# A two-layer diffusion trunk on one core: the context's out projection in one plain fp32 pass, and two modulation blocks moved to the end of the first MoE

## The chip, the cores and the metric

The kernel runs on one core of one Trainium2 chip. The metric is the device time of one execution in microseconds (us), the median over several executions. TensorE (PE), VectorE (DVE), ScalarE (ACT), GpSimd (POOL) and SyncE (SP) each work through a queue of their own in order; SP here only issues transfers (DMAs), and POOL nearly only that.

## The reference

Two layers; each has a mixer (attention, retention and a gated recurrence side by side, then one out projection) and a mixture of 16 experts. 512 latent tokens pass through both layers; 256 context tokens need the full way only in layer 0. What the change touches, cut down:

```python
# modulation, per layer: six vectors of 1024 for the latents and six for the context
sh1, sc1, g1, sh2, sc2, g2 = split(silu(c) @ mod_w[i] + mod_b[i], 6)
h = rms(x, norm1_g[i]) * (1 + sc1) + sh1
mix = concat([att, ret, lru]) @ w_out[i]          # 1024 x 1024, latents and (layer 0) context
x = x + g1 * mix                                  # all of it in float32
x = x + g2 * experts(rms(x, norm2_g[i]) * (1 + sc2) + sh2)
```

## The kernel before, in words

**Split products.** Large projections are computed in `fp32r`, a cheaper matmul format: each operand is split into a rounded high part (ACT copy) and the remainder (DVE subtract), and `mm3` (L414) adds three products, high by high, high by low and low by high. Weights are split by `split` (L406, lines L410 and L411 of the trace, tile `ws`); mixer outputs by `mix_split` (L905). Other matmuls take plain fp32 operands, without a split: the experts, the router, the gates of the recurrence (L554, L555).

**Out projection.** The mixer leaves its result transposed: `mx_l` (8 feature blocks of 128 by 512 latents) and `mx_c` (8 by 256 context tokens). Output columns go in four groups of 256. Because feature blocks 4 and 5 come last, the projection is in two runs: `out1` (L985) over blocks 6, 7, 0, 1, 2, 3 for all four groups, and `out2` (L1003) over blocks 4, 5, which also transposes the finished tokens (L1022), forms the router's logits (L1031) and sums squares (L1001). Each run adds its product, times the gate, onto the tokens (`out_unit`, L901 and L903). The latents go first; the context then goes through both runs again with weights loaded and split anew.

**Order around it.** `outer` (L1123) does the latents' `out2`, then their `route` (softmax, top-k in rounds of MAX8, FIND_INDEX8 and MATCH_REPLACE8 on DVE, L1090 to L1093, then small PE transposes L1100 and L1101 and the index list `gl`), then the context's projection, then the first experts. The scaled tokens `xo` (L1075) are written to DRAM (`xh_l`) and gathered back by index (`gath`, L1189), transposed (`gT`, L1198), and feed gate and up matmuls of expert 0 (`gu`, L1236). The frame the kernel is built in has a scheduler: it orders every engine's queue itself by priority and data, so the context's projection and the latents' routing interleave.

**Modulation.** `mod_block` (L265) makes one of the six vectors: eight loads of 512 KB on SP, four pairs of them multiplied (macc, L276) with a DVE add after each pair (L279). It is cut into steps, and `hook` (L425) puts one step into each projection unit of a mixer, as long as steps are left. Layer 0's mixer does its own blocks 2 to 5 and layer 1's 0 and 1; layer 1's mixer does its own 2 to 5, that is 16 steps.

**Weights of the experts.** `load_experts` (L1208) asks for 2 MB pieces on SP as the nine buffers of a ring come free. After the first MoE, layer 1 reads its tokens back (`load_x`, L342), norms them (L357, L363, L365), transposes (L374) and starts its first projection (`pf`).

Of the kernel before, what the change touches and what calls it, by code (L numbers as in the profile page):

```python
# [12 lines left out]
F32 = mybir.dt.float32  # L13
# [7 lines left out]
P = 128  # L21
L = 512
# [32 lines left out]
RP_QG, RP_QP, RP_KG, RP_KP, RP_LAM, RP_DEC, RP_N = 0, 64, 128, 192, 256, 512, 520  # L55
PR = {"ev": 0, "macc": 0, "tmp": 0, "aT": -60, "rw": 20, "rs": 20}
XW = 776
SW = 771
# [7 lines left out]
class Trunk:  # L66
# [198 lines left out]
    def mod_block(self, m, c):  # L265
# [3 lines left out]
        for k0 in range(0, KD, 2):  # L269
            acc = self.pj("macc")  # L270
            for k in range(k0, k0 + 2):
                wt = self.t(("mw", "mw", "k4")[self.mj % 3], [1024], "mw")
                self.mj += 1
                nc.sync.dma_start(wt, a["mod_w"][i, c, k])
                for q in range(4):
                    nc.tensor.matmul(acc[32 * q:32 * q + 32, :256], self.scT[:, k, :], wt[:, q * 256:(q + 1) * 256],  # L276
                                     start=k == k0, stop=k == k0 + 1)
            with self.pr("macc"):
                nc.vector.tensor_tensor(rs, rs, acc[:, :256], op=ALU.add)  # L279
            if k0 < KD - 2:  # L280
                yield
        n, v = divmod(c, 3)
        if v == 2:
            nc.sync.dma_start(m["gr"][n], rs)
        else:
            pt = self.pj("mT")
            for bb in range(2):
# [4 lines left out]
            for s in range(2):  # L292
# [3 lines left out]
                else:  # L296
                    nc.vector.tensor_copy(o, pv[:, :, :, s])
        yield
# [588 lines left out]

    def out_unit(self, g, tp, ks, w, g1, xs):
        nc = self.nc
        p = self.pj("op")  # L890
        hi, lo = self.ms[tp // 2]
        for n, k in enumerate(ks):
            for t in range(2):
                o = (tp % 2) * 256 + t * P
                self.mm3(p[:, t * 256:(t + 1) * 256], hi[:, k, o:o + P], lo[:, k, o:o + P],
                         w[n][:, 0], w[n][:, 1], n == 0 and t == 0, n == len(ks) - 1 and t == 1)
        o = g * 256
        tmp = self.t("q2", [2, 256], "tmp")
# [5 lines left out]

    def mix_split(self, s, a, b):  # L905
        src = (self.mx_l, self.mx_c)[s][:, a:b]
        hi, lo = (x[:, a:b] for x in self.ms[s])
        self.nc.scalar.activation(flat(hi), flat(src), AF.Copy)  # L908
        self.nc.vector.tensor_tensor(flat(lo), flat(src), flat(hi).bitcast(F32), op=ALU.subtract)  # L909

    def mixer(self, i, m, mn, xsrc, xres):
# [60 lines left out]
        g1 = self.gate1(m, ctx)  # L972
        self.ms = [[self.t("big", [KD, L], "m" + w, F32R) for w in "hl"]]
        xs = self.load_x(*xres, nc.gpsimd, ctx=False)
        tabs = self.ret_tables((2, 3), [self.t("w6", [1536], "tab") for _ in range(2)])
        self.ret_core(1, kq1, tabs, ctx)
        for k in (6, 0, 2):
            self.mix_split(0, k, k + 2)
        for n, _ in enumerate(self.out1(i, 0, xs[:4], g1)):
            if n == 3:  # L980
                self.flush()
                self.mix_split(0, 4, 6)
        return xs, g1

    def out1(self, i, s, xs, g1):  # L985
        nc, a = self.nc, self.a
        K1 = [6, 7, 0, 1, 2, 3]
        for g in range(4):
            w = []
            for h in range(2):  # L990
                raw = self.t("mw" if h else "w4", [3, 256], "wo")
                nc.sync.dma_start(raw, a["wo1"][i, g, h])
                w += [self.split(raw[:, k], k, "ws") for k in range(3)]
            for tp in range(2 * s, 2 * s + len(xs) // 2):
                self.out_unit(g, tp, K1, w, g1, xs)
                yield
# [6 lines left out]
    def out2(self, i, s, xs, g1):  # L1003
        nc, a = self.nc, self.a
        tps = range(2) if s == 0 else range(2, 3)
        nt = len(xs)
# [3 lines left out]
        for g in range(4):  # L1010
            if g % 2 == 0:
                raw = self.t("xsl" if i == DEPTH - 1 else "w4", [2, 2, 256], "wo")
                nc.sync.dma_start(raw, a["wo2"][i, g // 2])
            w = [self.split(raw[:, g % 2, k], k, "ws") for k in range(2)]
            for tp in tps:
                self.out_unit(g, tp, (4, 5), w, g1, xs)
            if g == 3:
# [105 lines left out]
    def outer(self, i, m, xs, xsrc, g1, free, base_l, base_c):  # L1123
# [118 lines left out]

    def experts(self, i, m, st, first, base_l, base_c):
        nc = self.nc
# [33 lines left out]
        if late is not None:  # L1278
            late()
        self.fixed = False  # L1280

    def pe(self, ins):
# [61 lines left out]
def emit(ctx, tc, a, out):  # L1344
# [4 lines left out]
    for i in range(DEPTH):  # L1349
        last = i == DEPTH - 1  # L1350
        base = (out, None) if last else (k.xr_l, k.xr_c)
        with ExitStack() as cw:
# [22 lines left out]
            k.open(cw, b=(4, 1), d=(2, 1))  # L1375
            k.experts(i, ms[i], st, xl, *base)
        src = base
# [90 lines left out]
```

## Time and profile before

| what | us |
|---|---|
| median of 3 executions | 2016.27 (2015.25 to 2017.24) |
| profiled execution, its time | 2015.42 |
| its span, first to last instruction | 2013.7 |
| PE busy | 1824.0 |
| DVE busy | 823.0 |
| ACT busy | 586.4 |

Layer 0's mixer fills the span to about 480 us, the context's projection and routing lie at 480 to 560, the first MoE at 560 to 1076, layer 1's mixer up to about 1530, and the second MoE after it. In the trace a plain fp32 matmul appears as two records (the experts' 32 gate and up matmuls as x64), an fp32r matmul as one. A bracket behind a row gives the idle time of its engine just before it and what ended that.

### The profile page before, as it was taken

To read this page: it belongs to the slowest core of one execution; us is meant where nothing else is said; L and a number is where in the kernel's file an instruction comes from. 1 tells how busy PE (TensorE), PEld (TensorE's weight loads), DVE (VectorE), ACT (ScalarE), POOL (GpSimd) and SP (SyncE) were. 2 spreads that over 40 slices of the span, in tenths; PEclk is the share of its full clock that TensorE was granted. 3 is DMA by queue.
4 is the path that set the end of the run, shared out by engine and by line. 5 is a ranking of instruction groups with operands and counts; after the bars stand their busy time and mean duration, and the time that the engine had idled before them with its cause. 6 is when DMAs were issued, how large, how long until landed. Compare 5 with 4: busy or idle time off the path is not lost.

```text
span 2013.7 us, 28802 instructions
## 1 busy us (share of the span) xinstructions
PE 1824.0 (91%) x11900; PEld 1058.1 (53%) x11900; DVE 823.0 (41%) x2016; ACT 586.4 (29%) x1240; POOL 119.2 (6%) x118
## 2 busy tenths in 40 slices
PE   6999999999799999999996989999985997878776
PEld 5788888677433333333333778986762422222222
DVE  5797876676610101011104597976752100000000
ACT  5656465424210101011103565554330000000000
POOL 0000000000010111011000000000000000000000
PEclk9999999999699999999997989999987999999999
DMA  8352433246499999999985543211448999999997
GB/s 311 131 188 83 160 113 112 83 161 254 165 373 403 404 402 404 411 403 402 397 348 191 176 149 104 73 33 58 177 192 355 417 417 417 423 417 416 424 418 275
DMA packets 76403, 545.62 MB, mean 271 GB/s; under 512 B 8720, under 2 KB 15008, under 8 KB 51952
## 3 DMA queue, kind: packets, MB, share of 16 engines
q1 hardware_dynamic: 61312, 501.26, 62.6%
q0 software_dynamic: 14960, 42.53, 7.1%
q8 instruction: 93, 1.52, 0.3%
q14 instruction: 38, 0.31, 0.0%
HBM read 522.25 MB, written 21.50 MB: 270 GB/s over the span
## 4 chain that ended last, share of the span: by engine, by line
PE 36%; issue 29%; DMA 21%; DVE 7%; ACT 3%; POOL 3%; POOLq 0%; SPq 0%; ACTq 0%; DVEq 0%
DMA w<-wu 6%; DMA w<-wg 6%; DMA w<-wd 4%; PE gu L1236 4%; PE pt L416 3%; PE pt L418 2%; PE pt L417 2%; PE ao L839 2%; PE pf L416 2%; PE pf L417 2%; PE pf L418 2%; DMA xh_l<-xo 2%; PE ro L727 2%; PE macc L276 2%; PE oe L1321 1%
## 5 line engine op out<-in xcount | busy, mean ns | idle before, releaser
L1236 PE MATMUL gu<-w,xsT 128*64 128x512 f32 x2048 | 476.4, 617 | 50.6 <-DMA w<-wu 32.8
L1236 PEld LDWEIGHTS gu<-w,xsT 128*64 128x64 f32 x2048 | 153.4, 142 | 350.9 <-issue 271.0
L1321 PE MATMUL oe<-w,hid 128*64 128x512 f32 x1024 | 234.6, 610 | 9.7 <-ACT hid L1306 9.6
L1240 DVE TENSOR_TENSOR hid<-hid,gu 128x512 f32<-128x512 f32 x32 | 22.0, 687 | 462.9 <-ACT hid L1239 462.9
L1239 ACT ACTIVATE hid<-gu 128x512 f32<-128x512 f32 x32 | 19.1, 597 | 526.0 <-PE gu L1236 526.0
L1321 PEld LDWEIGHTS oe<-w,hid 128*64 128x64 f32 x1024 | 74.3, 140 | 157.1 <-issue 138.6
L417 PE MATMUL pt<-ws,hh 128*128 128x256 f32 x448 | 127.9, 285 | 5.0 <-DVE ws L411 5.0
L416 PE MATMUL pt<-ws,hh 128*128 128x256 f32 x448 | 130.8, 292 | 0.0
L418 PE MATMUL pt<-ws,hl 128*128 128x256 f32 x448 | 128.1, 286 | 0.0
L1324 DVE SCALAR_TENSOR_TENSOR ob<-oe,afl,g 128x512 f32<-128x512 f32 x32 | 24.0, 751 | 221.4 <-PE oe L1321 221.4
L1293 PE MATMUL guc<-w,xsT 128*32 128x512 f32 x1024 | 113.2, 594 | 0.0
L410 ACT ACTIVATE ws<-wraw 128x256 fp32r<-128x256 f32 x192 | 72.8, 411 | 83.6 <-PE pt L418 31.9
L416 PEld LDWEIGHTS pt<-ws,hh 128*128 128x128 f32 x448 | 85.8, 191 | 9.1 <-issue 8.6
L411 DVE TENSOR_TENSOR ws<-wraw,ws 128x256 fp32r<-128x256 f32 x192 | 76.7, 419 | 33.6 <-ACT ws L410 33.2
L417 PEld LDWEIGHTS pt<-ws,hh 128*128 128x128 f32 x448 | 85.7, 191 | 5.7 <-DVE ws L411 5.5
L418 PEld LDWEIGHTS pt<-ws,hl 128*128 128x128 f32 x448 | 85.8, 191 | 0.1
L1205 ACT ACTIVATE xsT<-gT,ab 128x128 f32<-128x128 f32 x80 | 36.6, 458 | 144.2 <-PE gT L1198 116.8
L416 PE MATMUL op<-ws,mh 128*128 128x256 f32 x256 | 74.9, 293 | 3.1 <-ACT mh L908 3.1
L817 ACT ACTIVATE p<-sc,mx 128x768 f32<-128x768 f32 (+1 forms) x80 | 65.2, 816 | 33.9 <-DVE mx L815 30.5
L417 PE MATMUL op<-ws,mh 128*128 128x256 f32 x256 | 74.0, 290 | 0.0
L418 PE MATMUL op<-ws,ml 128*128 128x256 f32 x256 | 73.5, 289 | 0.3 <-DVE ml L909 0.3
L815 DVE TENSOR_REDUCE mx<-sc 128x1 f32<-128x768 f32 (+1 forms) x80 | 66.4, 847 | 10.8 <-PE sc L811 10.2
(385 smaller groups left out, 3187.1 us busy)
## 6 DMA issues: line engine op xcount, KB each, us to landing
w<-wg SPq DMA_DIRECT2D x63, 2048.0 KB, 26.4
w<-wd SPq DMA_DIRECT2D x63, 2048.0 KB, 22.9
w<-wu SPq DMA_DIRECT2D x62, 2048.0 KB, 16.1
mw<-mod_w SPq DMA_DIRECT2D x80, 512.0 KB, 4.3
wraw<-w_in SPq DMA_DIRECT2D x48, 512.0 KB, 3.6
wo<-wo SPq DMA_DIRECT2D x24, 384.0 KB, 3.5
mw<-mod_a SPq DMA_DIRECT2D x16, 512.0 KB, 10.7
xh_l<-xo POOLq DMA_DIRECT2D x8, 512.0 KB, 12.4
```

What stands on the lines that cost most here:

```text
L276: nc.tensor.matmul(acc[32 * q:32 * q + 32, :256], self.scT[:, k, :], wt[:, q * 256:(q + 1) * 256], start=k == k0, stop=k == k0 + 1)
L410: nc.scalar.activation(t[:, 0], src, AF.Copy)
L411: nc.vector.tensor_tensor(t[:, 1], src, t[:, 0].bitcast(F32), op=ALU.subtract)
L416: nc.tensor.matmul(out, lh, rh, start=first, stop=False)
L417: nc.tensor.matmul(out, lh, rl, start=False, stop=False)
L418: nc.tensor.matmul(out, ll, rh, start=False, stop=last)
L727: nc.tensor.matmul(ol[64 * h:64 * h + 64, :], v, ws[h][:, :L], start=t == 0, stop=t == 5)
L815: nc.vector.tensor_reduce(mx, s[:, :n], axis=AX.X, op=ALU.max, negate=True)
L817: nc.scalar.activation(ptl[m][:, :n], s[:, :n], AF.Exp, bias=mx, accum_out=sm[:, m, t:t + 1])
L1236: self.pe(nc.tensor.matmul(d[64 * h:64 * h + 64, j, :], xl[:, k, x0:x0 + CAPL], W(j, k)[:, h * 512:(h + 1) * 512], start=k == 0, stop=k == ...
L1293: self.pe(nc.tensor.matmul(dc[32 * q:32 * q + 32, :], xc[:, k, c0:c0 + CAPC], W(q // 2, k)[:, (q % 2) * 512:(q % 2) * 512 + 512], start=k ...
L1321: self.pe(nc.tensor.matmul(o[64 * h:64 * h + 64, :], hid[:, 1, c * P + hh * 64:c * P + hh * 64 + 64], W(2, k)[:, h * 512:(h + 1) * 512], s ...
```

## The change

It has two parts, which share only the file.

1. The context's projection no longer splits anything. `out_unit_c` loads the weights of a group (three pieces: 384, 384 and 256 KB) and runs all eight feature blocks in one accumulation of plain fp32 matmuls, then one gated add. The context's `out1` run, its 16 half-tensor splits and its 32 weight splits are gone, and so is the buffer `mc`. 192 fp32r matmuls of 256 columns become 64 plain ones.
2. Blocks 2 and 3 of layer 1's modulation leave layer 1's mixer. `mod_bulk` computes them at the end of the first MoE: four loads of 2 MB into the experts' buffers, 32 matmuls each in one accumulation, one add each. Layer 1's mixer has 8 steps left.

```diff
+    def mod_bulk(self, m, cs):
+        for c in cs:
+            rs = self.t("ob", [512], "mrow")[:, :256]
+            nc.gpsimd.dma_start(rs, a["mod_b"][i, c])
+            acc = self.b("macc")
+            for h in range(2):
+                wt = self.t(WTAGS[i - 1][self.nw % len(WTAGS[i - 1])], [4, D], "mwt")
+                self.nw += 1
+                nc.sync.dma_start(wt, a["mod_w"][i, c, 4 * h:4 * h + 4].rearrange("k p e -> p k e"))
+                for k in range(4 * h, 4 * h + 4):
+                    for q in range(4):
+                        nc.tensor.matmul(acc[32 * q:32 * q + 32, :256], self.scT[:, k, :],
+                                         wt[:, k % 4, q * 256:(q + 1) * 256], start=k == 0, stop=k == KD - 1)
+            nc.vector.tensor_tensor(rs, rs, acc[:, :256], op=ALU.add)
+            self.mod_out(m, c, rs, self.b)
...
     def side_work(self, m, mn):
-        for c in range(2, 6):
+        for c in range(2 if mn is not None else 4, 6):
             yield from self.mod_block(m, c)
...
+    def out_unit_c(self, i, g, g1):
+        w = []
+        for h in range(2):
+            raw = self.t("mw" if h else "w4", [3, 256], "wo")
+            nc.sync.dma_start(raw, a["wo1"][i, g, h])
+            w += [raw[:, k] for k in range(3)]
+        raw = self.t("ring", [2, 256], "wo")
+        nc.sync.dma_start(raw, a["wo2"][i, g // 2][:, g % 2])
+        w += [raw[:, k] for k in range(2)]
+        p = self.pj("op")
+        for n, k in enumerate(K1 + K2):
+            for t in range(2):
+                nc.tensor.matmul(p[:, t * 256:(t + 1) * 256], self.mx_c[:, k, t * P:(t + 1) * P], w[n],
+                                 start=n == 0 and t == 0, stop=n == KD - 1 and t == 1)
+        self.residual(g, 2, p, g1)
...
         for g in range(4):
+            if s:
+                self.out_unit_c(i, g, g1)
+            else:
...
-            mc = self.t("big", [2, KD, C], "mc", F32R)
-            self.ms.append([mc[:, 0], mc[:, 1]])
...
-            if s:
-                for k in (6, 0, 2, 4):
-                    self.mix_split(1, k, k + 2)
-                for _ in self.out1(i, 1, x, g1):
-                    pass
...
         self.fixed = False
+        if mn is not None:
+            self.mod_bulk(mn, (2, 3))
```

`mod_out` is the tail of `mod_block` made a function: block 2 (a gate) is stored to DRAM (`gr`) by SP, block 3 is transposed and copied. `residual` is the tail of `out_unit`.

The queues of instructions, as the scheduler leaves them, at the three places that the prediction speaks of. **DVE, the start of the latents' top-k**, before (`ws` is a split weight, `tmp` and `xc` the context's gated add, `tk`, `iu` and `pw` belong to the top-k):

```order
L1090 MAX tk_5459<-pw_5451 48x8
L411 TENSOR_TENSOR ws_5724<-wo_5722,ws_5724 128x256
L1091 MAX_INDEX iu_5460<-tk_5459,pw_5451 48x8
L411 TENSOR_TENSOR ws_5727<-wo_5722,ws_5727 128x256
L1093 MATCH_REPLACE pw_5451<-tk_5459,pw_5451 48x256
L411 TENSOR_TENSOR ws_5730<-wo_5722,ws_5730 128x256
```

and now:

```order
L945 TENSOR_TENSOR xc_5145<-xc_5145,tmp_5541 128x2x256
L1133 MAX_INDEX iu_5459<-tk_5458,pw_5450 48x8
L1135 MATCH_REPLACE pw_5450<-tk_5458,pw_5450 48x256
L126 COPY xT_972_5547<-xT_971_5544 128x256
L1132 MAX tk_5458<-pw_5450 48x8
```

Between the first MAX and the last of the eight rounds there were 11 splits of weights; none is left, and of the gated adds two pairs are there instead of five.

**SP, the loads of the context's weights** (`wo`) among the experts' first weights (`w`) and the write of the latents (`xr_l`), before:

```order
L992 DMA wo_5711<-wo 128x768
L1223 DMA w_5949<-wu 128x4096
L1184 DMA xr_l<-xl_4488 128x1024 x4
L992 DMA wo_5722<-wo 128x768
L1013 DMA wo_5775<-wo 128x1024
L1013 DMA wo_5853<-wo 128x1024
L1223 DMA w_5951<-wd 128x4096
```

and now:

```order
L1258 DMA w_5704<-wu 128x4096
L1219 DMA xr_l<-xl_4488 128x1024 x4
L925 DMA wo_5602<-wo 128x768
L925 DMA wo_5604<-wo 128x768
L925 DMA wo_5642<-wo 128x768
L925 DMA wo_5644<-wo 128x768
L1258 DMA w_5706<-wd 128x4096
```

The loads of groups 0 and 1 now stand ahead of these rows; those of groups 2 (wo_5602, wo_5604) and 3 wait for PE to be done with groups 0 and 1, and the down weights `wd` stand behind them.

**SP, the end of the first MoE**, before (`xl` and `xc` are layer 1's tokens, `wraw` its first weights):

```order
L1223 DMA w_8564<-wd 128x4096
L403 DMA wraw_8973<-w_in 128x1024
L403 DMA wraw_8975<-w_in 128x1024
L171 DMA gw_9276<-gatew 128x1024
L268 DMA mrow_9017<-mod_b 128x256
L403 DMA wraw_9123<-w_in 128x1024
L403 DMA wraw_9125<-w_in 128x1024
L274 DMA mw_9060<-mod_w 128x1024
L274 DMA mw_9106<-mod_w 128x1024
L342 DMA xl_8788<-xr_l 128x1024 x4
```

and now:

```order
L1258 DMA w_8319<-wd 128x4096
L296 DMA mwt_8500<-mod_w 128x4x1024
L296 DMA mwt_8518<-mod_w 128x4x1024
L296 DMA mwt_8541<-mod_w 128x4x1024
L296 DMA mwt_8559<-mod_w 128x4x1024
L308 DMA gr_98<-mrow_8497 128x256
L365 DMA xl_8629<-xr_l 128x1024 x4
L365 DMA xc_8630<-xr_c 128x1024 x2
L426 DMA wraw_8814<-w_in 128x1024
L426 DMA wraw_8816<-w_in 128x1024
```

The reads of the tokens now stand behind the store of block 2's result, and layer 1's first weights behind the tokens. On POOL the row of `mod_b` for block 3 stands ahead of the last scatter into the context.

## Rows read from the trace of the kernel before

**Rows 1.** Windows by stage: context stage, first MoE. Columns as named in the answer's head.
```profile
480.00:560.00 80.00, 65.06 (x343) 41.71 (x343) 47.28 (x187) 22.53 (x57) 8.36 (x13) 0.79 0.64 236
560.00:1076.00 516.00, 515.13 (x3733) 186.91 (x3731) 63.22 (x118) 57.86 (x119) 57.10 (x40) 1.00 0.98 389
```

**Rows 2.** Timeline of PE in the context stage: start, duration, engine, line, operation, idle.
```profile
488.69 0.28 PE L416 MATMUL op<-ws,mc 128*128 128x256 f32 x1
...
495.10 0.28 PE L416 MATMUL op<-ws,mc 128*128 128x256 f32 x1
...
504.77 0.58 PE L416 MATMUL op<-ws,mc 128*128 128x256 f32 x1 [4.63 <-ACT ws L410]
```

**Rows 3.** Timeline of ACT in the context stage.
```profile
503.26 1.15 ACT L1075 ACTIVATE xo<-xl,n2r 128x1024 f32<-128x1024 f32 x1 [7.44 <-DMA xh_l<-xo]
```

**Rows 4.** DVE by line, 497 to 524 us: count, busy us, mean ns, idle before.
```profile
L411 DVE TENSOR_TENSOR ws<-wo,ws 128x256 fp32r<-128x256 f32 x11 | 4.4, 404 | 4.6 <-ACT ws L410 4.6
...
L1090 DVE MAX8 tk<-pw 48x8 f32<-48x256 f32 x8 | 3.3, 412 | 0.0
L1091 DVE FIND_INDEX8 iu<-tk,pw 48x8 uint32<-48x256 f32 x8 | 3.3, 410 | 0.0
L1093 DVE MATCH_REPLACE8 pw<-tk,pw 48x256 f32<-48x256 f32 x7 | 2.8, 401 | 0.0
```

**Rows 5.** Timeline of all engines, from the latents' index list to expert 0.
```profile
530.95 1.01 POOL L1189 DMA_INDIRECT gath<-xh_l,gl  x1 [25.71 <-DVE gl L1116]
...
537.99 1.94 PE L1198 MATMUL gT<-ident,gath 128*128 128x128 f32 x8 [3.48 <-DMA gath<-xh_l,gl]
...
541.46 7.11 PE L1236 MATMUL gu<-w,xsT 128*64 128x512 f32 x18 [0.98 <-ACT xo L1075]
...
549.78 9.66 PE L1236 MATMUL gu<-w,xsT 128*64 128x512 f32 x44
```

**Rows 6.** Timeline of PE in layer 1: plain fp32 matmuls with a full 128x128 operand.
```profile
1148.30 0.60 PE L555 MATMUL gate<-u,gw 128*128 128x259 f32 x2
1148.74 1.02 PE L554 MATMUL gate<-u,gw 128*128 128x512 f32 x2
```

**Rows 7.** Windows in the context stage; the column before the DMA share is the granted clock.
```profile
530.00:545.00 15.00, 9.54 (x34) 4.95 (x36) 9.70 (x50) 5.14 (x12) 3.15 (x5) 0.50 0.62 239
```

**Rows 8.** DMA issues, 440 to 560 us: count, KB each, median us to landing.
```profile
wo<-wo SPq DMA_DIRECT2D x6, 384.0 KB, 3.3
xr_l<-xl SPq DMA_DIRECT2D x4, 512.0 KB, 11.1
```

**Rows 9.** DMA issues of the whole span.
```profile
w<-wg SPq DMA_DIRECT2D x63, 2048.0 KB, 26.4
```

**Rows 10.** Timeline of all engines from the first MoE into layer 1.
```profile
1057.27 0.80 SPq L403 DMA_DIRECT2D wraw<-w_in  x2
...
1072.68 3.66 PE L1335 MATMUL oec<-w,hidc 128*32 128x256 f32 x64 [0.47 <-ACT hidc L1313]
...
1077.63 1.75 SPq L342 DMA_DIRECT2D xl<-xr_l  x4
...
1090.56 1.05 PE L374 MATMUL xT<-ident,xl 128*128 128x128 f32 x3 [14.22 <-DVE xl L363]
...
1095.43 0.80 PE L416 MATMUL pf<-hh,ws 128*128 128x512 f32 x1 [0.60 <-ACT hh L398]
```

**Rows 11.** Windows at the end of the first MoE.
```profile
1050.00:1057.00 7.00, 7.00 (x82) 2.98 (x78) 0.69 (x1) 0.60 (x1) 0.00 (x0) 1.00 0.20 73
```

**Rows 12.** Timeline of PE in layer 1: one modulation step between two projection matmuls.
```profile
1211.32 1.07 PE L276 MATMUL macc<-mw,scT 128*32 128x256 f32 x16
1212.32 0.38 PE L416 MATMUL pt<-ws,hh 128*128 128x256 f32 x1
```

**Rows 13.** Windows of layer 1's mixer in which removed steps lie.
```profile
1160.00:1200.00 40.00, 34.12 (x266) 28.02 (x265) 39.10 (x85) 29.33 (x44) 0.00 (x0) 0.94 0.47 161
1210.00:1253.00 43.00, 42.76 (x362) 37.63 (x361) 29.11 (x58) 21.81 (x49) 0.00 (x0) 1.00 0.38 106
```

More of the change, by code (lines that the diff above doesn't have):

```diff
@@ L56 @@
 PR = {"ev": 0, "macc": 0, "tmp": 0, "aT": -60, "rw": 20, "rs": 20}
+K1 = (6, 7, 0, 1, 2, 3)
+K2 = (4, 5)
 XW = 776
@@ L281, in mod_block, with mod_out @@
                 yield
+        self.mod_out(m, c, rs, self.pj)
+        yield
+    def mod_bulk(self, m, cs):
+        nc, a, i = self.nc, self.a, m["i"]
+        for c in cs:
[12 more added lines that the diff above has]
+            self.mod_out(m, c, rs, self.b)
+    def mod_out(self, m, c, rs, bank):
+        nc, i = self.nc, m["i"]
         n, v = divmod(c, 3)
@@ L285, in mod_block @@
         else:
-            pt = self.pj("mT")
+            pt = bank("mT")
             for bb in range(2):
@@ L297, in mod_block @@
                     nc.vector.tensor_copy(o, pv[:, :, :, s])
-        yield
     def side_work(self, m, mn):
-        for c in range(2, 6):
+        for c in range(2 if mn is not None else 4, 6):
             yield from self.mod_block(m, c)
@@ L886, in att_head, with out_unit, residual @@
         self.late.append(fin)
-    def out_unit(self, g, tp, ks, w, g1, xs):
-        nc = self.nc
+    def out_unit(self, g, tp, ks, w, g1):
         p = self.pj("op")
-        hi, lo = self.ms[tp // 2]
         for n, k in enumerate(ks):
             for t in range(2):
-                o = (tp % 2) * 256 + t * P
-                self.mm3(p[:, t * 256:(t + 1) * 256], hi[:, k, o:o + P], lo[:, k, o:o + P],
+                o = tp * 256 + t * P
+                self.mm3(p[:, t * 256:(t + 1) * 256], self.mh[:, k, o:o + P], self.ml[:, k, o:o + P],
                          w[n][:, 0], w[n][:, 1], n == 0 and t == 0, n == len(ks) - 1 and t == 1)
+        self.residual(g, tp, p, g1)
+    def out_unit_c(self, i, g, g1):
+        nc, a = self.nc, self.a
+        w = []
[12 more added lines that the diff above has]
+        self.residual(g, 2, p, g1)
+    def residual(self, g, tp, p, g1):
+        nc = self.nc
         o = g * 256
@@ L903, in out_unit, with mix_split @@
         nc.vector.tensor_tensor(xx, xx, tmp, op=ALU.add)
[L905 to L909, printed above, removed]
+    def mix_split(self, a, b):
+        src, hi, lo = (flat(x[:, a:b]) for x in (self.mx_l, self.mh, self.ml))
+        self.nc.scalar.activation(hi, src, AF.Copy)
+        self.nc.vector.tensor_tensor(lo, src, hi.bitcast(F32), op=ALU.subtract)
     def mixer(self, i, m, mn, xsrc, xres):
@@ L972, in mixer @@
         g1 = self.gate1(m, ctx)
-        self.ms = [[self.t("big", [KD, L], "m" + w, F32R) for w in "hl"]]
+        self.mh, self.ml = (self.t("big", [KD, L], "m" + w, F32R) for w in "hl")
         xs = self.load_x(*xres, nc.gpsimd, ctx=False)
@@ L977, in mixer, with out1 @@
         for k in (6, 0, 2):
-            self.mix_split(0, k, k + 2)
-        for n, _ in enumerate(self.out1(i, 0, xs[:4], g1)):
+            self.mix_split(k, k + 2)
+        for n, _ in enumerate(self.out1(i, g1)):
             if n == 3:
                 self.flush()
-                self.mix_split(0, 4, 6)
+                self.mix_split(4, 6)
         return xs, g1
-    def out1(self, i, s, xs, g1):
+    def out1(self, i, g1):
         nc, a = self.nc, self.a
-        K1 = [6, 7, 0, 1, 2, 3]
         for g in range(4):
@@ L993, in out1 @@
                 w += [self.split(raw[:, k], k, "ws") for k in range(3)]
-            for tp in range(2 * s, 2 * s + len(xs) // 2):
-                self.out_unit(g, tp, K1, w, g1, xs)
+            for tp in range(2):
+                self.out_unit(g, tp, K1, w, g1)
                 yield
@@ L1004, in out2 @@
         nc, a = self.nc, self.a
-        tps = range(2) if s == 0 else range(2, 3)
         nt = len(xs)
@@ L1010, in out2 @@
         for g in range(4):
[L1011 to L1016, printed above, removed]
+            if s:
+                self.out_unit_c(i, g, g1)
+            else:
+                if g % 2 == 0:
+                    raw = self.t("xsl" if i == DEPTH - 1 else "w4", [2, 2, 256], "wo")
+                    nc.sync.dma_start(raw, a["wo2"][i, g // 2])
+                w = [self.split(raw[:, g % 2, k], k, "ws") for k in range(2)]
+                for tp in range(2):
+                    self.out_unit(g, tp, K2, w, g1)
             if g == 3:
@@ L1241, in gate_up, with experts @@
         return hid
-    def experts(self, i, m, st, first, base_l, base_c):
+    def experts(self, i, m, mn, st, first, base_l, base_c):
         nc = self.nc
@@ L1375, in emit @@
             k.open(cw, b=(4, 1), d=(2, 1))
-            k.experts(i, ms[i], st, xl, *base)
+            k.experts(i, ms[i], None if last else ms[i + 1], st, xl, *base)
         src = base
```

## The prediction, made before the changed kernel was run

> **What bounds the kernel now.** I read windows by stage first. In the first MoE PE is busy 515.13 of 516 us at full clock; in the context stage, 480 to 560, it is busy 65.06 of 80 at a mean granted clock of 0.79, and DVE 47.28 [rows 1]. So the MoE is bound by PE, and whatever moves the end of expert 0's gate and up matmuls (`gu`) moves all experts behind it. The stage before it is bound by something else, which the timelines of its engines show. ACT starts `xo` at 503.26 after 7.44 us idle, for a buffer that a DMA to DRAM still reads [rows 3]. The splits of the context's weights stand behind it on ACT: PE stalls 4.63 us for one [rows 2] and DVE 4.6 us, in the midst of the latents' top-k [rows 4]. The chain then runs index list, gather (530.95), `gT` (537.99), `gu` (541.46 to 549.78 + 9.66 = 559.4) [rows 5].
>
> In layer 1's mixer two kinds of stretches hold the steps that go: at 1160 to 1200 DVE is full (39.10 of 40), at 1210 to 1253 PE is (42.76 of 43) [rows 13].
>
> 0.2% (4 us) is what a measurement of this kernel can tell from no change. The sum is made against the profiled execution's 2015.42 us; the median of the runs stands 0.85 above it, and that is added at the end.
>
> **Context stage: the projection.** 192 fp32r matmuls go, at (495.10 - 488.69) / 54 = 0.119 us each [rows 2], 22.8 us. 64 plain ones come. A plain matmul with a full operand and 259 columns takes 1148.74 - 1148.30 = 0.44 us [rows 6], so 0.43 for 256 columns and 27.5 us in all: PE's own work grows by 4.7. DVE loses 32 splits of 404 ns, 11 of which (4.4 us) lay between the rounds of the top-k, and with them the 4.6 us wait [rows 4].
>
> The top-k alone is some 3.3 + 3.3 + 2.8 us plus the gated adds [rows 4]. Without splits, without the wait, and started some 5 us sooner since one accumulation has fewer gated adds ahead of it, I put its end at 507 to 510, the index list at 511 to 514, and the gathered tokens about 7 us later (530.95 to 537.99 [rows 5]), at 518 to 521.
>
> PE then is what is late. Of its 65.1 us, 7.11 + 9.66 are `gu` [rows 5] and 22.8 the old projection: 25.5 is left. Part of that lies behind `gT`, and part is stretched by the granted clock of 0.50 between 530 and 545 [rows 7]; I count half, 13. PE reaches `gT` at 480 + 27.5 + 13 + 4 = 524.5, with 4 for waits, about the size of the one stall in rows 2. Before it was 538: 13.5 sooner. From `gT` to the end of `gu` it took 559.4 - 538 = 21.4 us, which would end it at 546. Three us I add for the clock: 18 records of `gu` took 7.11 us in the slow stretch, 44 took 9.66 later, so 0.395 against 0.22 each [rows 5], and the context's small transposes now stand within it. Were all 44 slow it would be 7.7 us. **-10 us, bounds -13.5 (same clock) and -5 (all slow).**
>
> The loads for groups 0 and 1 are asked for well ahead: 3.3 us to landing for 384 KB [rows 8]. The loads for groups 2 and 3 now wait for PE to be done with the buffers of 0 and 1. Per group PE has 27.5 / 4 = 6.9 us of work, and the next group covers the landing. They stand on SP behind the write `xr_l` (11.1 us to landing [rows 8], issued, not awaited), and the 2 MB `wd` behind them. I cost this at nothing; the cover is one group of matmuls plus the routing's transposes. If it goes, see the second rival.
>
> **Latents' stage.** The context's activations lose their splits: eight blocks of 256 columns at 404 ns [rows 4] are 3.2 us of DVE, most beside PE's work. -0.5 (0 to -1.5).
>
> **Start of layer 1.** The last output matmuls `oec` start at 1072.68 and end 3.66 later, at 1076.3 [rows 10]; they are 32 matmuls of 32 by 256, as each moved block is. The four 2 MB loads go into the experts' ring, whose buffers the last two experts free one by one; an expert takes 516 / 16 = 32 us [rows 1], so I estimate the loads' starts from 1044 or sooner to about 1061. DMA moves 73 GB/s with a share of 0.20 at 1050 to 1057 [rows 11], against 389 GB/s over the MoE [rows 1], at which 8 MB take 21 us. So I take the weights to be there. Block 2 then runs 1076.3 to 1080; after its add SP issues the store `gr` at about 1081, and only then the reads `xl`, which began at 1077.63 [rows 10]: +3.4. Block 3's matmuls lie in the 14.22 us in which PE waits for the normed tokens before `xT` [rows 10], and cost nothing; with that cover gone they would cost 3.7. POOL issues block 3's row of `mod_b` ahead of the context's last scatter, about one issue of 1.0 us [rows 5], partly beside the rest. Layer 1's first weights were asked for at 1057.27 [rows 10] and are now asked for behind `xl`; 384 KB land in 3.3 us [rows 8], but their splits now fall among the norm and `hh`, where they had been done ahead. **+4.5 in all, bounds +3 (the store alone) and +7 (3.4 + 1.0 + some six splits of 0.404).**
>
> **Layer 1's mixer.** Eight of 16 steps go, each 1212.32 - 1211.32 = 1.0 us of PE [rows 12]. Four lie where PE is the bound: -4.0. Four lie where DVE is full; there only the step's DVE add, by the nearest row 0.4 us [rows 4], comes back: -1.6. **-5.5, bounds -3 and -8 (each step in full).**
>
> Sum: -10 - 0.5 + 4.5 - 5.5 = -11.5, 2003.9 profiled, 2004.8 as median: **2005 us**. The bounds together give -13.5 - 1.5 + 3 - 8 = -20 (1996) and -5 + 7 - 3 = -1 (2015); that all fall on one side is unlikely, and the likeliest case's own range is 2000 to 2010.
>
> **Rivals.** First, the clock. Before, the granted clock was 0.50, the 1.2 GHz level, between 530 and 545, after PE had waited 4.63, 3.48 and more for others [rows 2, 5, 7]. If it falls at 503, when some 26 of the 64 plain matmuls are left, these take 0.86 each, +11; this takes the place of the 3 us: -13 + 11 - 0.5 + 4.5 - 5.5 = -3.5, 2012 profiled, **2013**. For it: routing gives PE gaps in the midst of the projection. Against it: the projection now waits for no split, so that it fills PE's gaps better than before. Chance 0.13. The Trainium skill, "TensorE: Matmul & The Clock Gate", section "HAM oscillation — how this bites in real kernels", says that bursts of matmuls with waits for data between them each begin cold, at half the clock. The stretch with 0.50 agrees; by that rule the plain matmuls behind each gap that the routing leaves run cold, and the time is this rival's.
>
> Second, slower. The loads of groups 2 and 3 wait for buffers and then land late because the experts' weights are in the queues. A 2 MB piece takes 26.4 us from issue to landing in the MoE [rows 9]. If group 2's pieces take that, against about 10 us of cover, PE and with it the routing behind it is 16 us late: -11.5 + 16 = +4.5, **2021**. It decides from a landing time of about 10 + 11.5 = 21 us on. For it: SP's new order. Against it: 3.3 and 11.1 us in rows 8, in the same stage, at a DMA share of 0.64 [rows 1]. Chance 0.07.
>
> Third, the removed steps of layer 1 give nothing, because DVE and ACT set the pace there and PE's full window only follows: -11.5 + 5.5 = -6, 2009.4 profiled, **2010**. For it: DVE at 39.10 of 40 just ahead [rows 13]. Against it: 42.76 of 43 on PE. Chance 0.10.
>
> **How the numbers follow.** Forecast 0.70, rivals 0.13, 0.07, 0.10. Faster by over 0.2% means below 2012.2. The forecast gives nearly all of its 0.70 (0.67), the third 0.09, the first 0.03: 0.79. Within 0.2%: the rest of the first, 0.10, and 0.03 of the others: 0.13. Slower: 0.08. The range, 1998 to 2014, leaves out the second rival, and about 0.1 at the ends.
>
> **What would show it.** Right: no `ws` on DVE and ACT at 497 to 524; `gT` some 13 us and `gu`'s end some 10 us sooner; `oec` end to `xT` 4 to 5 us longer than the 14.26 of rows 10; eight `macc` steps in layer 1's mixer, and 1160 to 1253 shorter by some 5. Wrong: a granted clock of 0.5 from 503 on (first rival), PE waiting for DMA `wo` in the projection (second), the mixer as long as before (third), or PE waiting for `mwt` behind `oec`, which I took to be there.

## The result, and the profile of the changed kernel

| | us |
|---|---|
| median after, 4 executions | 1989.22 (1987.90 to 1993.06) |
| median before, 4 executions | 2016.76 (2015.25 to 2017.75) |
| ratio, 95% interval | 0.9873 (0.9854 to 0.9891) |
| forecast | 2005, range 1998 to 2014 |
| profiled execution after, its span | 1993.06, 1991.3 |

The change makes the kernel 1.3% faster. The side was forecast, the size was not: 27.5 us by the medians against 11.5, outside the range. The profiled execution after is the slowest of its four; against the profiled one before it is 22.4 us shorter, and that difference can be taken apart stretch by stretch. In the table a stretch ends with the instruction named, in the profiled executions.

| stretch, and what ends it | before | after | difference | forecast |
|---|---|---|---|---|
| layer 0's mixer, to the first transpose of finished tokens | 461.9 | 462.2 | +0.3 | -0.5 |
| context stage, to the first `guc` | 99.6 | 86.7 | -12.9 | -10 |
| first MoE, to the last `oec` | 514.9 | 514.9 | 0 | 0 |
| start of layer 1, to its first `pf` | 19.1 | 24.4 | +5.3 | +4.5 |
| layer 1's mixer, to its last token transpose | 402.6 | 390.2 | -12.4 | -5.5 |
| routing and second MoE, to the last matmul | 504.4 | 505.7 | +1.3 | 0 |
| from the last matmul to the end | 11.2 | 7.1 | -4.1 | 0 |

So the missing 11 us lie in three places: the mixer (6.9), the end (4.1), the context stage (2.9); the others take 3 back.

**The context stage.** First its windows, of the whole stage and of layer 1's mixer, in the kernel before (length, PE, PEld, DVE, ACT, POOL, granted clock, DMA share, GB/s):

```profile
461.90:561.50 99.60, 84.26 (x464) 54.70 (x466) 61.75 (x213) 33.40 (x96) 9.11 (x14) 0.83 0.57 209
1095.43:1498.02 402.59, 390.19 (x2658) 317.94 (x2658) 294.25 (x658) 205.04 (x434) 5.45 (x10) 0.97 0.33 110
```

and the same two in the changed one:

```profile
462.20:548.90 86.70, 79.07 (x396) 48.82 (x394) 50.78 (x178) 24.16 (x69) 9.05 (x14) 0.96 0.70 265
1088.23:1478.40 390.17, 375.91 (x2528) 311.25 (x2528) 292.80 (x651) 205.13 (x437) 5.44 (x10) 0.97 0.29 96
```

A stretch of PE's is work at full clock, plus idle time, plus what the slow clock adds to the work. The granted clock is a mean over the whole stretch, idle time too, and a slow clock costs nothing while PE is idle; so its cost has to be read from the stretches that lie at 0.50. Windows of these, before:

```profile
502.39:509.22 6.83, 4.12 (x17) 3.82 (x18) 2.94 (x11) 4.52 (x12) 0.53 (x1) 0.50 0.91 326
519.46:546.77 27.31, 21.09 (x77) 11.27 (x78) 17.94 (x80) 9.25 (x26) 3.15 (x5) 0.50 0.45 165
```

and after:

```profile
525.98:532.81 6.83, 4.17 (x13) 1.32 (x14) 5.07 (x26) 3.94 (x5) 2.12 (x4) 0.50 0.68 256
```

At 0.50 I count half of PE's busy time as lost. This is an estimate and a little high: a record of `gu` takes 0.395 us in the slow stretch and 0.22 later [rows 5]. Before, the stage has 99.6 - 84.3 = 15.3 us idle and (4.12 + 21.09) / 2 = 12.6 lost to the clock, so 71.7 of work are left. After, 7.6 are idle, 2.1 lost, and 77.0 are work. The plain matmuls did add work, 5.3 us by this and 4.7 by the forecast; the gain is idle time (-7.7) and clock (-10.5).

Before, the clock falls while PE waits 4.63 us for a split [rows 2], is back at full speed from 509.22 to 519.46, and then lies at 0.50 until 546.77. This second stretch costs the most, 10.5 us, and PE's waits in the 10 us ahead of it are short, 1.20 us at most; what began it is not shown. After, the clock holds until PE is idle again, for the first stage of the context's routing. The timelines of POOL and PE of the changed kernel, which answer to [rows 5]:

```profile
510.37 1.02 POOL L1224 DMA_INDIRECT gath<-xh_l,gl  x1 [12.82 <-DVE gl L1158]
```

```profile
513.22 5.35 PE L933 MATMUL op<-wo,mxc 128*128 128x256 f32 x24
...
521.64 0.65 PE L1233 MATMUL gT<-ident,gath 128*128 128x128 f32 x4
...
528.64 0.62 PE L1125 MATMUL prT<-ident,pr 128*16 128x128 f32 x4 [4.66 <-DVE pr L1112]
529.18 4.57 PE L1271 MATMUL gu<-w,xsT 128*64 128x512 f32 x10
...
534.71 12.23 PE L1271 MATMUL gu<-w,xsT 128*64 128x512 f32 x54
```

The gather is asked for 20.6 us sooner (510.37 for 530.95), `gT` starts 16.4 sooner and `gu` ends 12.5 sooner (546.9 for 559.4). `gT` has no idle time ahead of it: PE's own queue reaches it last, as forecast.

**The start of layer 1**, the timeline of all engines, which answers to [rows 10]:

```profile
1060.16 3.66 PE L1372 MATMUL oec<-w,hidc 128*32 128x256 f32 x64 [0.47 <-ACT hidc L1350]
...
1063.63 7.09 PE L299 MATMUL macc<-mwt,scT 128*32 128x256 f32 x128
...
1066.74 0.60 POOL L291 DMA_DIRECT2D mrow<-mod_b  x1 [4.79 <-DMA xr_l<-ob,sl]
...
1067.79 0.34 SPq L308 DMA_DIRECT2D gr<-mrow  x1
1068.23 1.88 SPq L365 DMA_DIRECT2D xl<-xr_l  x4
...
1082.92 0.45 PE L397 MATMUL xT<-ident,xl 128*128 128x128 f32 x1 [11.21 <-DVE xl L386]
...
1088.23 0.80 PE L439 MATMUL pf<-hh,ws 128*128 128x512 f32 x1 [0.61 <-ACT hh L421]
```

Both blocks run without a gap behind the last `oec`, so their weights were there. The reads `xl` wait for the store `gr`, 4.4 us behind `oec`'s end instead of 1.3; and the row of block 3 (`mrow`) waits on POOL for the scatter of the latents.

### The profile page after: what moved, and what is told of

Same layout as the page of the kernel before. It is cut to its first block, busy times and chain, and to the rows that moved or that the text cites. A ratio compares the mean times of both kernels' runs of the same rounds, so it can differ in the third digit from the quotient of the medians.

```text
span 1991.3 us, 28552 instructions
## 1 busy us (share of the span) xinstructions
PE 1808.1 (91%) x11836; PEld 1048.9 (53%) x11836; DVE 805.6 (40%) x1966; ACT 572.3 (29%) x1204; POOL 120.5 (6%) x120
## 4 chain that ended last, share of the span: by engine, by line
PE 66%; DMA 20%; DVE 9%; ACT 3%; issue 2%; POOL 0%; POOLq 0%; SPq 0%; ACTq 0%; DVEq 0%
PE gu L1271 14%; PE oe L1358 7%; DMA w<-wu 6%; DMA w<-wg 6%; PE guc L1330 6%; DMA w<-wd 4%; PE oec L1372 3%; PE ao L862 2%; PE pt L439 2%; PE pt L441 2%; PE pt L440 2%; PE pf L439 2%; PE pf L440 2%; PE pf L441 2%; PE ro L750 2%
## 5 line engine op out<-in xcount | busy, mean ns | idle before, releaser
L1274 ACT ACTIVATE hid<-gu 128x512 f32<-128x512 f32 x32 | 19.1, 597 | 529.1 <-PE gu L1271 529.1
L441 PEld LDWEIGHTS pt<-ws,hl 128*128 128x128 f32 x448 | 86.7, 193 | 0.1
L838 DVE TENSOR_REDUCE mx<-sc 128x1 f32<-128x768 f32 (+1 forms) x80 | 66.2, 846 | 10.3 <-PE sc L834 9.7
## 6 DMA issues: line engine op xcount, KB each, us to landing
mw<-mod_a SPq DMA_DIRECT2D x16, 512.0 KB, 10.5
```

What stands on the lines that cost most here:

```text
L441: nc.tensor.matmul(out, ll, rh, start=False, stop=last)
L838: nc.vector.tensor_reduce(mx, s[:, :n], axis=AX.X, op=ALU.max, negate=True)
```

## Experiments

Each timing stands beside the kernel before on the same chip. Traces are compared with that of a second profile of the changed kernel (`after_again`) where nothing else is said.

**The change again, its parts alone, and the splits put back** (one chip).

> The changed kernel once more, with a second profile. The first profile had a granted clock of 0.95 and 0.94 between 120 and 150 us, where the kernel before had 1.00, and lost 1.5 us there, and its last write to DRAM ended 6.0 us after its issue where the one before ended 10.2 after. If these are chance of one execution, neither comes again and the median stays near 1989; if they belong to the change, both come again. Either way the rows from the context stage to layer 1's mixer should repeat within 1 us: expert 0's gate and up matmuls end 12 to 13 us earlier than in the kernel before, and layer 1's mixer is 10 to 12 us shorter.

1991.57 us against 2013.66, ratio 0.9891 (0.9875 to 0.9907). The two intervals for the change overlap from 0.9875 to 0.9891, which is 22 to 25 us. Context stage 86.7, start 23.4, mixer 390.3, from the last matmul to the end 7.2: all within 1 us of the first profile. The slow stretch at 133 us, 3.4 us long, did not come again there; one of the same length lies at 457 us instead, where the kernel before has one too (458 us), so its place is chance. The short end did come again, so that belongs to the change.

Part 1 alone is the changed kernel with

```diff
-        for c in range(2 if mn is not None else 4, 6):
+        for c in range(2, 6):
...
-        if mn is not None:
-            self.mod_bulk(mn, (2, 3))
```

> Part 1 alone: the context's projection in plain fp32, while blocks 2 and 3 of the modulation stay in layer 1's mixer. My forecast's terms give -10.5 for this part, so about 2006. What the two traces now show (context stage -12.8, latents' stage -1.6) gives -14.4, about 2002. If the whole gain of the change belonged to this part, it would be 1989.

2003.60 against 2013.66, 0.9959 (0.9946 to 0.9972): -10.1. Its context stage is 86.9 us long, its mixer 400.6, its end 11.3.

Part 2 alone is the kernel before with `mod_bulk`, `mod_out` and the new lower bound of the loop (cut down):

```diff
-        for c in range(2, 6):
+        for c in range(2 if mn is not None else 4, 6):
...
+        if mn is not None:
+            self.mod_bulk(mn, (2, 3))
```

> Part 2 alone: blocks 2 and 3 at the end of the first MoE, the context's projection as before. My forecast's terms give +4.5 - 5.5 = -1, about 2016. What the two traces now show (start of layer 1 +5.3, its mixer -11.6) gives -6.3, about 2010.5. If the parts add up, this run's and the other part's differences sum to that of the changed kernel, -27.5; what is missing from the sum is interplay.

2002.45 against 2013.66, 0.9948 (0.9934 to 0.9962): -11.2, where my terms gave -1. Start 23.9, mixer 389.3, end 7.0. The parts add up within their intervals (-21.3 against -22.1), and the size that I missed is part 2's. The context stage, whose projection is the old one here, is 97.6 us long; it has 17.5 us idle and 7.7 lost to the clock, for 15.3 and 12.6 in the kernel before, so the same queue does not always pay the same for the clock.

The splits put back, unread:

```diff
             w += [raw[:, k] for k in range(3)]
+            for k in range(3):
+                self.split(raw[:, k], k, "ws")
...
         w += [raw[:, k] for k in range(2)]
+        for k in range(2):
+            self.split(raw[:, k], k, "ws")
```

> The changed kernel, with the context's weights split all the same on ACT and DVE; nothing reads the splits. PE's work is that of the changed kernel, DVE's top-k again has 12 splits between its rounds. If the gain in the context stage came from taking the splits out of the chain (top-k, index list, gather), the index list, at 510 us now, falls to about 520, gT starts at about 527 instead of 521.6 and the run is 4 to 8 us slower than the changed kernel. If PE's work and its clock alone set the stage, the run is within 2 us of it.

1990.29, 0.9885 (0.9870 to 0.9901): no slower than the changed kernel. DVE by line, 488 to 512 us (count, busy, mean ns, idle before):

```profile
L434 DVE TENSOR_TENSOR ws<-wo,ws 128x256 fp32r<-128x256 f32 x14 | 5.7, 408 | 0.1
L1136 DVE MAX8 tk<-pw 48x8 f32<-48x256 f32 x8 | 3.3, 414 | 0.1
```

14 splits lie among the rounds again, 5.7 us of DVE, but nothing waits: 0.1 us, where [rows 4] had 4.6. The gather is asked for 50.9 us into the stage (511.87), for 48.2 in the changed kernel and 69.1 in the kernel before, and the stage is 85.6 us long. So the splits' own time on DVE and ACT is not what the old stage paid for. What is gone in both kernels is PE's waiting for them and most of the slow clock. (Unread, a split also frees its buffer at once, which one that PE reads does not; so this run keeps the splits' time and not their hold on the buffers.)

**Half of the projection's matmuls left out** (every second feature block).

```diff
         for n, k in enumerate(K1 + K2):
+            if n % 2:
+                continue
...
-                                 start=n == 0 and t == 0, stop=n == KD - 1 and t == 1)
+                                 start=n == 0 and t == 0, stop=n == KD - 2 and t == 1)
```

> The changed kernel with the context's projection over four of its eight feature blocks: the other four are left out, so 32 plain matmuls or 13.8 us of PE are missing. If PE's work ends the context stage, the latents' transposes gT come sooner until the gathered tokens are what is late: these were asked for at 510.4 and need some 6 to 8 us, so gT moves from 521.6 to about 517 and the run is 3 to 6 us faster than the changed kernel. If the chain of top-k and gather ends it, gT stays and the run is within 1.5 us of it. If nothing else were late, it would be 13.8 us faster.

1983.71 against 2015.14, 0.9847 (0.9830 to 0.9863). The context stage is 82.8 us long, 3.9 less, inside what was expected, but not in the way expected; by the ratios the whole run gains 8.9, with an uncertainty of 4.6. The timelines of PE and POOL:

```profile
520.92 1.94 PE L1235 MATMUL gT<-ident,gath 128*128 128x128 f32 x8 [7.13 <-DMA gath<-xh_l,gl]
```

```profile
515.81 1.02 POOL L1226 DMA_INDIRECT gath<-xh_l,gl  x1 [11.63 <-DVE n2r L139]
```

`gT` hardly moves and now waits 7.13 us for the gathered tokens, which are asked for at 515.81, 5.4 us later than in the first profile of the changed kernel. The gain is behind `gT`, since the context's small matmuls no longer stand between `gT` and `gu`. Taken apart as above, of 14.2 us less work (expected for 32 matmuls: 13.8) 7.8 came back as idle time and 2.7 as slow clock. Because the chain of top-k and gather itself came later here, this run does not say what a shorter projection would bring with that chain unmoved.

**Eight steps put back into layer 1's mixer**, in the hooks that the removed ones left empty, unused: matmuls without the add, the add without matmuls, and both.

```diff
+        if mn is None:
+            for c in range(2, 4):
+                yield from self.mod_dummy(m, c)
```

(`mod_dummy` is `mod_block` without its tail, and without the part that the run leaves out. It comes behind blocks 4 and 5, so the order is 4, 5, 2, 3, and not the old 2, 3, 4, 5.)

> The changed kernel, and in layer 1's mixer eight more steps in the places of the removed ones: their loads and their matmuls, without DVE's add and without use of the result. Theory A: PE's work is what the mixer is long for, also where DVE is full, since PE's idle time in it is the same 27 us in the kernel before and in the changed one; a step is worth 1.2 us of PE (1.0, and 0.1 before and behind it against the pitch of its neighbours), eight give back 9 to 10 us. Theory B (my forecast): four of the eight lie where DVE sets the pace and cost nothing without the add, so 4 to 5 us.

> The changed kernel, and in layer 1's mixer eight more steps with their loads and DVE's add alone (on loaded data), no matmuls, the result unused. Theory A (PE's work): within 2 us of the changed kernel. Theory B (DVE sets the pace in half of the places): 4 adds of 0.42 us and their waits come in full, 2 to 4 us. If it is the 8 MB of loads that cost, through the queue that issues them or the memory, both this and the run with the matmuls are slower by the same amount.

> The changed kernel, and in layer 1's mixer eight more steps with loads, matmuls and DVE's add together, the result unused. The steps with matmuls alone cost 5.2 us by the median (3.1 in the length of the mixer), those with adds alone 4.2 (3.5 in the mixer). If the two costs add up, this run is 6 to 9 us slower than the changed kernel. If they need each other, since matmuls alone fill idle time of PE and adds alone make idle time that matmuls would have filled, it is 10 to 12 us slower, as the mixer of the kernel with part 1 alone is 10.3 us longer than that of the changed one.

With matmuls 1996.78 (0.9906, 0.9889 to 0.9922), with adds 1995.78 (0.9902, 0.9886 to 0.9919), with both 1995.82 (0.9914, 0.9899 to 0.9930). The windows of the mixer, one kernel after the other:

```profile
1086.84:1480.24 393.40, 381.95 (x2656) 313.16 (x2656) 293.27 (x651) 205.57 (x437) 5.42 (x10) 0.98 0.33 116
```

```profile
1087.16:1480.98 393.82, 376.75 (x2528) 312.76 (x2528) 294.15 (x659) 204.75 (x437) 5.42 (x10) 0.97 0.34 116
```

```profile
1086.97:1481.60 394.63, 382.87 (x2656) 313.07 (x2656) 295.54 (x659) 205.11 (x437) 5.43 (x10) 0.98 0.34 116
```

The mixer grows by 3.1, 3.5 and 4.3 us. (The whole runs, by the ratios, by 3.0, 2.2 and 4.6, each with an uncertainty of 4.6.) By lengths alone Theory A, PE's work in full, seems to fall: matmuls cost 3.1 us and not 9 to 10. But a length hides what happened to idle time and clock. Taken apart as the context stage was, with half of PE's busy time in the stretches at 0.50 as the clock's loss, all mixers of layer 1 are:

| kernel, steps in layer 1's mixer | length | idle | lost to the clock | work at full clock |
|---|---|---|---|---|
| before, 16 | 402.6 | 12.4 | 11.7 | 378.5 |
| part 1 alone, 16 | 400.6 | 12.6 | 9.4 | 378.5 |
| part 1 alone, other order (below), 16 | 396.8 | 10.5 | 7.5 | 378.8 |
| changed, first profile, 8 | 390.2 | 14.3 | 9.3 | 366.6 |
| changed, second profile, 8 | 390.3 | 14.4 | 9.9 | 366.0 |
| with matmuls, 8 and 8 put back | 393.4 | 11.4 | 6.4 | 375.6 |
| with adds, 8 and 8 put back | 393.8 | 17.1 | 10.1 | 366.6 |
| with both, 8 and 8 put back | 394.6 | 11.8 | 6.6 | 376.2 |
| three blocks moved (below), 4 | 378.9 | 13.2 | 4.8 | 360.9 |
| four blocks moved (below), 0 | 374.9 | 12.7 | 6.9 | 355.3 |

Work at full clock goes by the number of steps: a block of four steps is 5.4 to 6.1 us of it, wherever it is taken out, and the order does not touch it. Against part 1 alone the changed kernel's mixer has 12.2 us less work (mean of two profiles), 1.8 more idle time and 0.2 more slow clock: the 10.3 us by which it is shorter, but for rounding. So Theory A holds for the work; the adds alone bring none of it back, only idle time. The matmuls put back bring 9 to 10 us of work back; that the mixer grows by 4.3 at most has another reason. Part 1 alone and the changed kernel both have a stretch of 10.2 us at 0.50, which begins 88 to 98 us into the mixer. The run with both has none, the one with matmuls 3.4 us. In the changed kernel, PE and the window of that stretch:

```profile
1179.49 1.12 PE L819 MATMUL aT<-ident,qk 128*128 128x128 f32 x4 [4.16 <-DVE qk L807]
```

```profile
1177.93:1188.17 10.24, 7.64 (x33) 6.95 (x34) 9.00 (x16) 7.45 (x13) 0.00 (x0) 0.50 0.32 104
```

In the run with both PE waits 1.53 us there (for `qk`, ahead of a step's matmuls), and the clock stays up. With these two gone it has 3.3 us less lost to the clock and 2.6 less idle than the changed kernel. Against part 1 alone its mixer is 6.0 us shorter: 2.8 of these are clock, 0.8 idle time, and 2.3 work, which can be the tails of the two blocks (the runs leave them out; that is not shown by itself).

What one step is on PE shows in the timeline of part 1 alone:

```profile
1195.84 0.28 PE L440 MATMUL pt<-ws,hh 128*128 128x256 f32 x1
1195.95 0.28 PE L441 MATMUL pt<-ws,hl 128*128 128x256 f32 x1
1196.16 1.07 PE L278 MATMUL macc<-mw,scT 128*32 128x256 f32 x16
1197.16 0.38 PE L439 MATMUL pt<-ws,hh 128*128 128x256 f32 x1
1197.38 0.28 PE L440 MATMUL pt<-ws,hh 128*128 128x256 f32 x1
```

Neighbours stand 0.12 apart; the step has 0.21 before it and the next matmul 0.22 behind it, so it takes 1.0 + 0.2 = 1.2 us out of PE's queue. I read 1.0 off [rows 12]. Eight times 1.2 is 9.6; the table has 9.0 to 10.2.

**The same 16 steps in another order** (part 1 alone, nothing removed).

```diff
-        for c in range(2, 6):
+        for c in ((2, 3, 4, 5) if mn is not None else (4, 5, 2, 3)):
```

> The kernel with part 1 alone, in which layer 1's mixer does its four modulation blocks in the order 4, 5, 2, 3 instead of 2, 3, 4, 5: the same 16 steps in the same hooks, nothing removed. In the queues the frequency sums (frs) of the recurrence then stand some 60 instructions later on PE, as in the changed kernel and in the one with eight steps put back. If the order that the scheduler leaves there is what made the mixer 6 us longer than the steps' own cost, the mixer is 393 to 397 us long instead of 400.6 and the run is 4 to 7 us faster than part 1 alone. If it was the work of blocks 2 and 3, it is within 1.5 us of part 1 alone.

1996.48 against 2015.29, 0.9904 (0.9889 to 0.9919), where part 1 alone had 0.9959. Its mixer, in windows:

```profile
1084.60:1481.42 396.82, 386.28 (x2658) 313.56 (x2658) 293.85 (x658) 204.44 (x434) 5.44 (x10) 0.98 0.33 112
```

396.8 us for 400.6, with no work removed. The two timelines show the place. Part 1 alone, PE and DVE:

```profile
1179.98 0.56 PE L440 MATMUL pt<-ws,hh 128*128 128x256 f32 x1 [3.88 <-DVE ws L434]
```

```profile
1187.39 0.17 DVE L624 TENSOR_SCALAR frv<-frs 128x8 f32<-128x8 f32 x1 [3.01 <-PE frs L621]
```

and with the order changed, PE and DVE:

```profile
1182.10 0.39 PE L440 MATMUL pt<-ws,hh 128*128 128x256 f32 x1 [0.81 <-DVE ws L434]
```

```profile
1193.68 0.17 DVE L624 TENSOR_SCALAR frv<-frs 128x8 f32<-128x8 f32 x1 [1.19 <-PE frs L621]
```

In the old order PE waits 3.88 us for a split that DVE has behind other work, its clock falls, and then DVE waits 3.01 us for sums (`frs`) that the slowed PE makes. In the new order these sums stand some 60 instructions later on PE, and the clock stays up. The window of 10 us, in the old order and in the new:

```profile
1180.00:1190.00 10.00, 9.11 (x41) 8.82 (x42) 6.96 (x31) 1.05 (x2) 0.00 (x0) 0.50 0.18 54
```

```profile
1180.00:1190.00 10.00, 9.04 (x74) 8.39 (x71) 9.94 (x22) 6.49 (x11) 0.00 (x0) 1.00 0.66 223
```

So the order that the scheduler leaves when steps move can be worth some us by itself: 3.8 by the mixers of two profiles, 2.1 of idle time and 1.9 of clock. The ratios of the two kernels differ by more, 11 us with an uncertainty of 4, and which is nearer is not settled. But it is not what the changed kernel gained: there PE stalls 4.16 us at that place, for `qk` instead of a split, and its clock is at 0.50 for 10.2 us all the same.

**Two loads on POOL** (part 1 alone, with the two rows of `mod_b` loaded by POOL at the end of the first MoE, unread).

```diff
+        if mn is not None:
+            for c in (2, 3):
+                rs = self.t("ob", [512], "mrow")[:, :256]
+                nc.gpsimd.dma_start(rs, self.a["mod_b"][mn["i"], c])
```

> The kernel with part 1 alone, with POOL's two loads of rows of mod_b at the end of the first MoE as in the changed kernel, unread; nothing else of part 2. The last drain of POOL took 9.6 to 9.7 us in both kernels without part 2 and 5.3 to 5.4 in all with it. If the two more DMAs on POOL's queue make that difference, the time from the last matmul to the end falls from 11.3 to about 7.1 us here and the run is about 4 us faster than part 1 alone. If it comes from the time at which the last scatter is issued, or from the rest of part 2, it stays at 11.3.

2001.68 against 2015.29, 0.9931 (0.9917 to 0.9944), 5.6 us better than part 1 alone by the ratios, with an uncertainty of 3.8. The time from the last matmul to the end is 7.0 us, for 11.3 in part 1 alone. The program's last line on POOL (durations in ns: least, median, most) in the kernel before, the changed one, and this one:

```profile
L1464 POOLq DRAIN  x3: 46/103/9567, 2003.3 to 2013.4; - x3
```

```profile
L1501 POOLq DRAIN  x3: 46/103/5380, 1985.1 to 1991.0; - x3
```

```profile
L1503 POOLq DRAIN  x3: 46/103/5262, 1989.1 to 1994.9; - x3
```

The last drain takes 9.57 us before and 5.38 and 5.26 with two more DMAs on POOL in the middle of the program. These alone bring 4 us, 900 us later. It is not the data: the last write lands 4.7 to 4.8 us after its issue in all three. Why two more DMAs on that queue change its last drain is not shown.

**A better start of layer 1, and more blocks moved.** The store of block 2 goes to POOL behind the last scatter, and the rows of `mod_b` into another buffer (cut down):

```diff
-            rs = self.t("ob", [512], "mrow")[:, :256]
+            rs = self.t("hidc", [768], "mrow")[:, :256]
...
-            nc.sync.dma_start(m["gr"][n], rs)
+            (eng or nc.sync).dma_start(m["gr"][n], rs)
```

> The changed kernel with the store of block 2's result issued by POOL behind the last scatter instead of by SP ahead of layer 1's token reads, and with the two rows of mod_b in buffers that do not wait for the scatter of the latents. If the store on SP is what holds the reads back (they began 4.4 us after the last output matmul, 1.3 in the kernel before), the start of layer 1 comes 3 us sooner and the run is 2 to 4 us faster than the changed kernel. If the reads wait for the landing of the last scatter, it is within 1 us.

1988.00 against 2015.14, 0.9868 (0.9851 to 0.9884). The reads are asked for 2.1 us behind `oec` instead of 4.4, and the start is 21.3 us long for 23.4. That is shown in the trace; by the intervals this kernel and the changed one can't be told apart (0.9891 and 0.9873).

With blocks (2, 3, 4) and with (2, 3, 4, 5) moved, otherwise the same:

> Block 4 moved to the end of the first MoE too, with block 2's store on POOL; four steps are left in layer 1's mixer. Four steps fewer give 5 us by the 10.3 that eight gave. The block's 3.7 us of matmuls go into PE's 10.7 us of idle time ahead of layer 1's first transposes, and its two loads of 2 MB are asked for before layer 1's tokens. So about 4 us faster than the run with the store on POOL alone; if the loads hold up the token reads, no faster.

> Blocks 4 and 5 moved too, with the stores on POOL; no step is left in layer 1's mixer. Eight steps fewer give 10 us by the same price. 7.3 us of matmuls go into the 10.7 us of idle time, but 16 MB of weights, 40 us at the 400 GB/s of the first MoE, now stand ahead of the token reads on SP, and the last two wait for buffers that the last output matmuls free. If these hold up the reads by less than 10 us, this is the fastest version, by up to 8 us against the run with the store on POOL alone; if by more, slower than that run.

1990.40 and 1990.70 against 2012.93, both 0.9891. The mixer falls to 378.9 and 374.9 us, the start grows to 31.6 and 38.9: start and mixer together 410.5 and 413.8, for 409.7 with two blocks. The timeline of PE with four blocks:

```profile
1076.37 3.64 PE L299 MATMUL macc<-mwt,scT 128*32 128x256 f32 x32 [3.63 <-DMA mwt<-mod_w]
...
1082.35 3.27 PE L299 MATMUL macc<-mwt,scT 128*32 128x256 f32 x32 [1.10 <-DMA mwt<-mod_w]
```

The cover that two blocks find, four do not: their loads land late and stand ahead of the tokens. Two blocks are about the right number.

## Why the prediction was right and wrong

- **What bounds the context stage, and that PE reaches `gT` last**: right. Forecast 524.5 for `gT` and 511 to 514 for the index list; 521.6 and 510.1 came.
- **-10 us there**: right in its kind, too small by 2.9. The term that was too large is PE's way to `gT`, "480 + 27.5 + 13 + 4". From 480 to `gT` 41.6 us passed and not 44.5: PE was idle for 2.2 of the 4 set aside for waits, and the projection and the rest took 39.4 of the 40.5, all at full clock. The price of 0.43 us a matmul held (24 records, 12 matmuls, in 5.35 us). The "three us I add for the clock", behind `gT`, came out nearly in size, but as idle time: from `gT` to the end of `gu` it took 25.3 us, 3.9 more than before; PE waits 4.66 us for the context's routing in it, and the clock costs 2.1 there, less than before.
- **The loads of groups 2 and 3 at no cost**: right, no matmul waits for one.
- **+4.5 at the start of layer 1**: right, +5.3 and +4.3 in the two profiles, by the store and the reads as described; the weights were there.
- **-5.5 in the mixer**: here the sum failed most, and by its mechanism. The -1.6 for the four steps that "lie where DVE is full", of which only the DVE add was to come back, took PE's work there for covered; a step went in at 1.0 us where it is 1.2, and the blocks' tails had no term. The runs show that all of the removed PE work came back: some 12 us, more than the bound of -8, "each step in full". Less slow clock added 2.4 to that and more idle time took 1.9 back, and the mixer became 12.4 us shorter in the first profile. That the steps put back cost 4.3 us, near the 5.5, is luck and no support: with them a stall and a slow stretch went away.
- **Nothing at the end**: wrong by 4.1 us. POOL's loads were weighed by their place in the queue, and their effect on the last drain could not be read from the trace of before.
- **The rivals.** The clock rival had the sign reversed. It also put the 0.50 between 530 and 545 down to waits of which one, the 3.48 us ahead of `gT`, came after: the clock had been there since 519.46. The rule cited from the Trainium skill, "TensorE: Matmul & The Clock Gate", "HAM oscillation — how this bites in real kernels", agrees with the trace where PE waits long: the clock falls to 0.50 within the 4.63 us stall before, and within the 4.66 us gap after. I applied it to the new kernel only, while it was the old one that paid more. The rival of late loads did not come, nor did the third: the mixer gave more, not nothing.
- **The range** took its lower end from known terms only. The two pieces that put the result outside it are the price of the steps, which its bound did not reach, and the drain, an effect of two loads on work 900 us later.

## What to carry to other kernels

Take a PE stage apart into work at full clock, idle time and what the slow clock costs while PE is busy, before pricing a change and again before explaining one: a format that does more work but waits for no other engine can win by the other two. Do the same to the runs that put a step back. When a scheduler orders the queues, a step that moves has two prices, its own work and a new order around it; a difference in length mixes them, and here the order hid most of the work. And compare what comes after the last instruction too.

## What was not expected of the hardware

The clock's low stretches come partly by chance: one of 3.4 us at 0.50 lies near 133 us in the first profile of the changed kernel and near 457 us in its second. Others belong to the kernel: 10.2 us at 0.50 in layer 1's mixer come in the kernel before, in both profiles of the changed one and in those of part 1 and part 2 alone, each time with a PE stall of 3.9 to 4.2 us. In the three runs that have matmuls in the order 4, 5, 2, 3 the stalls at that place are 1.6 us at most, and 3.4 us or nothing lie at 0.50. POOL's last drain took 9.6 us in the kernel before and 5.3 to 5.4 in the kernels with a few more DMAs on POOL at the end of the first MoE; its cause stays open.
